# First mixer of a two-block layer: the gate row's sums and the gate on the output projection move from GpSimd to VectorE

## The chip, the cores and the metric

The kernel runs on one core of a Trainium2 chip. The metric is the device time of one execution in microseconds, as the median of several runs. The engines are TensorE (matmul and its weight loads), VectorE, ScalarE (called ACT in the rows), GpSimd (POOL) and SyncE (SP), whose queue issues nearly all DMA transfers of weights. Each engine works through its own instructions in order and waits for the others by semaphores.

## What is computed

Two transformer blocks run one after the other on 256 tokens of 1024 features, all in float32. The first block modulates: six rows of 1024 come from one condition vector, and two of them are gates on the outputs of the block's two halves.

```python
def first_block(x, c, w_ada, b_ada, ...):
    mod = (silu(c) @ w_ada + b_ada)                 # 1024 x 6144 weights
    shift_m, scale_m, gate_m, shift_f, scale_f, gate_f = split(mod, 6)
    h = rms_norm(x, g_mix) * (1 + scale_m) + shift_m
    x = x + gate_m * hybrid_mixer(h, ...)           # two attentions, 8 heads each
    h = rms_norm(x, g_ffn) * (1 + scale_f) + shift_f
    x = x + gate_f * hierarchical_moe(h, ...)       # 32 experts, 2 per token
    return rms_norm(x, g_final)

def hybrid_mixer(h, w_in, b_forget, g_out_a, g_out_b, w_out):
    proj = h @ w_in                                 # 1024 x 2896
    ...
    o = concatenate([rms_norm(oa, g_out_a), rms_norm(ob, g_out_b)])
    return o @ w_out                                # 1024 x 1024
```

`oa` is an attention with a choice of 64 keys per query (an indexer makes the choice), `ob` a forgetting attention. The second block has a recurrent mixer and a dense feed-forward part.

## The kernel before, in words

Tokens lie in two blocks of 128 (t = 0, 1). Products that need accuracy are made from two parts, `hi` (rounded by ACT) and `lo` (the rest, by VectorE), in three matmuls (`mm3`); `split` makes the parts of a weight piece of 128x1024.

Weights come in pieces of 1 MB through a ring of eleven buffers (`raw`), by loads that SP issues in the order of the program: `load` (L53) and, for the modulation rows, `ada_piece` (L125), four pieces `wada` for each row. The order is the string at L207: a digit is a piece of that modulation row (0 and 1 are loaded before), "bq", "aq", "kv" and so on are pieces of w_in. Behind it come the four pieces of w_out (`wob` for the forgetting attention's half, `woa` for the other) and then the expert weights (`load_experts`), which go into this ring and two smaller ones. The smaller ones share space with the first mixer's tiles, so the last loads before the experts begin wait for the mixer's end; the twenty-first waits for the buffer of `xn2`, the normed input of the experts.

The modulation rows 0 to 4 are made by TensorE (`ada`, L328). Row 5, `gate_f`, is made otherwise (`gate_row`, L360): for each of the eight halves of its pieces, ACT scales 128x1024 weights by the column of silu(c) in place (L366), and GpSimd adds them to `modrow[:, 1]` (L367); `gate_row_end` (L370) sums over the partitions with a matmul of ones, within the first expert unit. `modrow[:, 0]` is `gate_m`. The gate is put on the weights of the output projection: `gate_out` (L378) multiplies the w_out pieces by `modrow[:, 0]` on GpSimd (L382), `wob` in `gate_out(0)` and `woa` in `gate_out(1)`. `proj_out` (L575) then makes the products of each half, and `add` (L585) scales the result by the attention's norm and adds it to `xt`, the running sum.

The work of the first mixer is written as generators, one for each job, and a string at L879 says in which order their steps are written out: "B" and "C" are the forgetting attention on token block 0 and 1 (`attn`, L694, with the softmax in L732 to L747), "D" and "E" the other attention, "2", "3", "4" the modulation rows on TensorE, "5" `gate_row`, "G" and "H" `gate_out`, "o" and "p" the output projection's halves, lower case letters projections. A scheduler then lays out each engine's instructions ahead of time by this order as priority; an instruction that is ready may come ahead of earlier ones that are not. Only SP's loads and what is marked so keep the order of the program. `mm` has one line for all matmuls (L100), and `hilo` one for each part (L86, L87), so groups are told apart by their tiles.

Of the kernel before, what the change touches and what calls it, by code (L numbers as in the profile page):

```python
# [7 lines left out]
FT = mybir.dt.float32  # L8
# [3 lines left out]
AF = mybir.ActivationFunctionType  # L12
OP = mybir.AluOpType
# [3 lines left out]
T = 256  # L17
# [15 lines left out]
def tile_block(ctx: ExitStack, tc: tile.TileContext, A, out):  # L33
    nc = tc.nc
    pe, act, dve, pool = nc.tensor, nc.scalar, nc.vector, nc.gpsimd
# [10 lines left out]
    def bank(shape, name):  # L46
        return ps.tile(shape, FT, name=name, tag="bank")
# [22 lines left out]
    def load_cols(name, dname, width, c0, n, j0, nj):  # L70
        return load(name, (nj, n), dram(dname, j0 * width + c0,
                                        [[8 * width, 128], [width, nj], [1, n]]))
# [3 lines left out]
    def held(ins):  # L76

        if holding:
            tc.keep_in_program_order(ins)
        return ins  # L80
# [8 lines left out]
    def split(src, name, n, eng=dve):  # L89
        hi = spl.tile([128, 1024], FR, name=name + "h", tag="hi")[:, :n]  # L90
        lo = spl.tile([128, 1024], FR, name=name + "l", tag="lo")[:, :n]
        hilo(hi, lo, src, eng)
        return hi, lo
# [16 lines left out]
    def mm3(o, lh, rh, start, stop):  # L110
        mm(o, lh[0], rh[0], start, False)
        mm(o, lh[0], rh[1], False, False)
        mm(o, lh[1], rh[0], False, stop)
# [11 lines left out]
    def ada_piece(v):  # L125
        w = wada.setdefault(v, [])
        q = len(w)
        w.append(load(f"wada{v}_{q}", (2, D), dram("w_ada", 2 * q * 6 * D + v * D,
                                                   [[8 * 6 * D, 128], [6 * D, 2], [1, D]])))
# [6 lines left out]
    xt = const.tile([128, 2, D], FT, name="xt")  # L136
    modrow = const.tile([128, 2, D], FT, name="modrow")
# [5 lines left out]
    a1 = p1.enter_context(tc.tile_pool(name="a1", bufs=1, side="right"))  # L143
# [8 lines left out]
    bkT, bv = bkv[:, 0], bkv[:, 1].rearrange("p a b -> p (a b)").rearrange("p (t n) -> p t n", t=2)  # L152
# [51 lines left out]
    later = {"bq": w_bq, "bk": w_bk, "bv": w_bv, "aq": w_aq}  # L204
    for v in (2, 3, 5, 4):
        wada[v] = []
    for name in 'bq bq bk 2 2 bk bv bv 3 5 aq kv 2 2 3 3 aq 3 5 5 5 4 4 4 4'.split():  # L207
        if name == "kv":
            w_kv = load_cols("wkv", "w_in", WIN, 512, 256, 0, 8)
        elif name in COLS:  # L210
            c0, n = COLS[name]
            k = len(later[name])
            later[name].append(load_cols(f"win{c0}_{k}", "w_in", WIN, c0, n, 4 * k, 4))
        else:
            ada_piece(int(name))
    wo = []

    def wob_load():
        for i in range(2):
            wo.append(load(f"wob{i}", (2, D), dram("w_out", (512 + 256 * i) * D,  # L220
                                                  [[D, 128], [128 * D, 2], [1, D]])))
# [4 lines left out]
    W, last = {}, []  # L226
# [94 lines left out]
    cs = const.tile([128, 8], FT, name="cs")  # L321
# [38 lines left out]
    def gate_row():  # L360

        m = modrow[:, 1]
        for q in range(4):
            for jj in range(2):
                w = wada[5][q][:, jj]
                act.activation(w, w, AF.Copy, scale=cs[:, 2 * q + jj:2 * q + jj + 1])  # L366
                pool.tensor_tensor(m, m, w, op=OP.add)  # L367
            yield

    def gate_row_end():  # L370
# [4 lines left out]
        for half in range(2):  # L375
            act.activation(m[:, 512 * half:512 * half + 512], b[half], AF.Copy)

    def gate_out(part_):  # L378

        for r in range(4):  # L380
            w = wo[2 * part_ + r // 2][:, r % 2]
            pool.tensor_tensor(w, w, modrow[:, 0], op=OP.mult)  # L382
        yield


    def rstd_of(ssq, n, name, post=None):
        t = small.tile(list(ssq.shape), FT, name=name + "s", tag="ns")
        held(act.activation(t, ssq, AF.Sqrt, bias=epsc[:, 0:1], scale=1.0 / n))
        r = post if post is not None else small.tile(list(ssq.shape), FT, name=name + "r", tag="nr")
        dve.reciprocal(r, t)  # L390
        return r

    def sumsq(src, name, junk):
        s = small.tile([128, 1], FT, name=name)
        act.activation(junk, src, AF.Square, accum_out=s)
        return s
# [38 lines left out]
    for t in range(2):  # L435
        r = rstd_of(sumsq(xt[:, t], "ss", xn[:, t]), D, "rs")
# [121 lines left out]
    def turn_x(t):  # L558
        b = [bank([128, 4, 128], "p_tr") for _ in range(2)]
        for j in range(8):  # L560
            held_pe(pe.transpose(b[j // 4][:, j % 4], xt[:, t, j::8], ident))
        return b
# [4 lines left out]
    def first_half_first(n, last):  # L567

        if n == last - 2:
            return [(n, 0)]  # L570
        if n == last - 1:
            return [(n, 0), (n - 1, 1), (n, 1)]
        return [(n, 0), (n, 1)]

    def proj_out(part_, oh, ol, rs):  # L575
        acc, kept = [], []
        for r in range(4):
            def cut(r=r):
                return split(wo[2 * part_ + r // 2][:, r % 2], "wo", 1024)

            def prod(hi, lo, r=r):
                if r == 0:
                    acc.extend([bank([128, 512], "p_wo") for _ in range(2)] for _ in range(2))
                kept.append((hi, lo))
                def add(t, half):  # L585
                    hs = slice(half * 512, half * 512 + 512)
                    held(dve.scalar_tensor_tensor(xt[:, t, hs], acc[t][half], rs[:, t:t + 1], xt[:, t, hs],
                                                  op0=OP.mult, op1=OP.add))

                if part_ and r == 3:  # L590
                    holding.extend([True, True])
                for r_, t in first_half_first(r, 4):
                    ts = slice(t * 128, t * 128 + 128)
                    hi, lo = kept[r_]
                    for half in range(2):
                        hs = slice(half * 512, half * 512 + 512)
                        mm3(acc[t][half], (oh[:, r_, ts], ol[:, r_, ts]), (hi[:, hs], lo[:, hs]), r_ == 0, r_ == 3)
                        if part_ and r == r_ == 3:
                            if t == 0:
                                add(t, half)  # L600
                            elif half == 0:
                                trb.append(turn_x(0))
                if r == 3:
                    if part_:
                        del holding[:]
                        add_outs.append(add)
                    else:
                        for t in range(2):
                            for half in range(2):
                                add(t, half)  # L610

            yield cut, prod
# [210 lines left out]
    def flush():  # L823
        while pend:
            pend.pop(0)()
# [6 lines left out]
    def loads1():  # L832
        wob_load()
        woa_load()
        load_experts(len(RING) - RING.count(3))
        yield

    def turn_rows():
        p_rows = bank([128, 64], "p_rows")
        pe.transpose(p_rows, rows, ident[:64, :64])  # L840
        dve.tensor_copy(cols, p_rows)
        yield

    def rstd_b():
        oa.extend([a1.tile([128, 4, T], FR, name="oaT", tag="iq"), a1.tile([128, 4, T], FR, name="oaL", tag="bq")])
        rstd_of(ssq[:, 2:4], 512, "rb_", rsb)
        yield

    def rstd_a():
        rstd_of(ssq[:, 0:2], 512, "ra_", rsa)  # L850
        yield

    def router_weights():
# [3 lines left out]
        for j in range(8):  # L857
# [15 lines left out]
            "a": proj_fm(w_aq, aqT, 0.125, perm=True), "n": proj_kv(), "o": proj_out(0, obT, obL, rsb),  # L873
            "F": forget(), "X": indexer(1), "Y": indexer(0), "B": attn("b", 0), "C": attn("b", 1),
            "D": attn("a", 0), "E": attn("a", 1), "2": ada(2), "3": ada(3), "4": ada(4), "5": gate_row(),
            "G": gate_out(0), "H": gate_out(1), "T": turn_rows(), "W": loads1(), "R": rstd_b(), "S": rstd_a(),
            "Z": router_weights()}
    p_ = None
    for c in "iiqikqqFqXFXbbYYbbvY5TXXF22XY25XY5v5vYXYXv2BWBa2aaBYBnGB3BC33CCCC3BCanB3C!CR4D4D4D4E4DDDEoEHoEoDEoDEEESZpppp":  # L879
        if c == "!":  # L880
            flush()
        elif c == "p":
            if p_ is None:
                p_ = proj_out(1, *oa, rsa)
            main([next(p_)], 0)
        elif c.islower():
            main([next(work[c])], 0)
        else:
            next(work[c])
# [475 lines left out]
    q = const.tile([128, 2], FT, name="q")  # L1365
# [475 lines left out]
    q = const.tile([128, 2], FT, name="q5")  # L1841
# [36 lines left out]
    q = small.tile([128, 2], FT, name="ss5q")  # L1878
# [28 lines left out]
    for half in range(2):  # L1907
# [10 lines left out]
                                  op0=OP.mult, op1=OP.mult))  # L1918
# [31 lines left out]
```

## Time and profile before

| | |
|---|---|
| timed runs, median (lowest to highest of 3) | 741.2 us (740.72 to 742.93) |
| the profiled execution | 738.99 us, span 737.2 us |
| TensorE busy | 660.9 us, 90% of the span |
| VectorE busy | 402.3 us, 55% |
| ACT busy | 311.4 us, 42% |
| GpSimd busy | 88.9 us, 12% |
| moved by DMA | 196.94 MB, mean 267 GB/s |

The profile is one execution of the program. Its span runs from the first to the last instruction; the execution's own time is longer by what lies around it. A busy share is an average over stages with different limits: the first mixer takes the first 186 us, the experts the stretch up to some 414 us, the second block the rest. "Releaser" names what ended a wait. Where GpSimd's busy time stands, 42.5 us of it are the sums and gate products of this change (19.9 for L367, 11.8 and 10.8 for L382).

### The profile page before, as it was taken

The page shows a single profiled execution, that of the slowest core. Times are in us where ns is not written, and L with a number is a line of the kernel's source. Part 1 is how long each engine was busy: PE and PEld are TensorE (multiplying, and loading weights), DVE is VectorE, ACT ScalarE, POOL GpSimd, SP SyncE. Part 2 cuts the span into 40 slices and gives each one's busy share as a digit, 9 for nine tenths or more (in the row PEclk, how much of TensorE's full clock was granted, in tenths as well). Part 3 has the DMA queues.
Part 4 walks back from the last instruction along what each step waited for, and adds up shares of the span by engine and source line. Part 5 has one row for each costly group of instructions (what it writes and reads, how often), then busy time and mean ns, then how long its engine had stood idle before and what let it go on. Part 6 is the DMA issues. An engine that isn't in the chain of part 4 may idle for free. (4 is left out here: it accounts for less than half of the span.)

```text
span 737.2 us, 13263 instructions
## 1 busy us (share of the span) xinstructions
PE 660.9 (90%) x5489; PEld 510.4 (69%) x5489; DVE 402.3 (55%) x737; ACT 311.4 (42%) x513; POOL 88.9 (12%) x87
## 2 busy tenths in 40 slices
PE   5799996999899775998876989999999999999996
PEld 1498774877765333444442489987899999898994
DVE  2367978575663230423312269959676555555555
ACT  1446556564741010201110177685455444444445
POOL 7010309910000000000000063010000000000001
PEclk9899998999989998999988999999999999999999
DMA  9999779995639899998999999653445555550001
GB/s 342 372 382 359 257 273 292 307 405 206 261 133 421 322 421 415 405 397 332 422 418 420 374 370 387 212 172 116 138 149 172 172 192 201 177 199 34 1 1 57
DMA packets 69203, 196.94 MB, mean 267 GB/s; under 512 B 7550, under 2 KB 33219, under 8 KB 57350
## 3 DMA queue, kind: packets, MB, share of 16 engines
q1 hardware_dynamic: 67558, 195.30, 70.5%
q8 instruction: 53, 0.87, 0.5%
q10 hardware_dynamic: 1216, 0.30, 0.2%
q0 software_dynamic: 352, 0.28, 0.1%
q14 instruction: 24, 0.20, 0.1%
HBM read 194.81 MB, written 1.05 MB: 266 GB/s over the span
## 5 line engine op out<-in xcount | busy, mean ns | idle before, releaser
L100 PE MATMUL p_gu<-Xl,wguh 128*128 128x256 f32 x352 | 99.8, 284 | 0.0
L100 PE MATMUL p_gu<-Xh,wgul 128*128 128x256 f32 x352 | 99.3, 283 | 0.0
L100 PE MATMUL p_gu<-Xh,wguh 128*128 128x256 f32 x352 | 98.9, 283 | 0.1
L100 PEld LDWEIGHTS p_gu<-Xl,wguh 128*128 128x128 f32 x352 | 67.5, 192 | 0.5
L100 PEld LDWEIGHTS p_gu<-Xh,wguh 128*128 128x128 f32 x352 | 67.1, 192 | 0.7 <-ACT Xh L1379 0.4
L100 PEld LDWEIGHTS p_gu<-Xh,wgul 128*128 128x128 f32 x352 | 67.4, 192 | 0.3 <-DVE wgul L87 0.2
L100 PE MATMUL p_gu<-eg,xg 128*32 128x256 f32 x576 | 41.8, 416 | 15.3 <-PEq L1296 9.5
L87 DVE TENSOR_TENSOR wdnl<-wdn,wdnh 128x1024 fp32r<-128x1024 f32 x22 | 27.0, 1225 | 32.4 <-ACT wdnh L86 32.4
L100 PEld LDWEIGHTS p_gu<-eg,xg 128*32 128x32 f32 x576 | 19.7, 118 | 36.0 <-issue 24.4
L1149 DVE TENSOR_TENSOR sl<-sl,p_gu 128x256 f32<-128x256 f32 x9 | 3.8, 422 | 69.2 <-ACT sl L1148 69.2
L1148 ACT ACTIVATE sl<-p_gu 128x256 f32<-128x256 f32 x9 | 3.5, 384 | 87.9 <-PE p_gu L100 87.9
L100 PE MATMUL p_w<-hTh,wih 128*128 128x256 f32 x128 | 37.7, 297 | 2.5 <-ACT wih L86 2.5
L100 PE MATMUL p_dn<-ed,aT 128*32 128x512 f32 (+2 forms) x304 | 34.5, 573 | 5.2 <-ACT aT L1156 5.0
L86 ACT ACTIVATE wdnh<-wdn 128x1024 fp32r<-128x1024 f32 x22 | 23.3, 1058 | 36.5 <-PE p_gu L100 35.9
L87 DVE TENSOR_TENSOR wgul<-wup,wguh 128x1024 fp32r<-128x1024 f32 x22 | 27.0, 1226 | 21.3 <-ACT wguh L86 20.2
L1066 ACT ACTIVATE xg<-p_xg,modcol,af 128x128 f32<-128x128 f32 x36 | 15.6, 462 | 53.2 <-DVE xg L1068 53.0
L87 DVE TENSOR_TENSOR wgul<-wgt,wguh 128x1024 fp32r<-128x1024 f32 x22 | 27.0, 1225 | 19.8 <-ACT wguh L86 19.8
L86 ACT ACTIVATE wguh<-wgt 128x1024 fp32r<-128x1024 f32 x22 | 23.3, 1061 | 33.7 <-PE p_gu L100 18.2
L100 PE MATMUL p_w<-Xh,w2h 128*128 128x256 f32 x128 | 37.0, 289 | 0.5 <-ACT w2h L86 0.4
L100 PE MATMUL p_w<-Xh,w2l 128*128 128x256 f32 x128 | 36.3, 285 | 1.1 <-DVE w2l L87 0.6
L100 PE MATMUL p_w<-hTl,wih 128*128 128x256 f32 x128 | 36.9, 289 | 0.0
L100 PE MATMUL p_gu<-eu,xg 128*32 128x256 f32 x576 | 35.2, 379 | 1.9 <-DMA eu<-in_w_up_dram 1.9
(625 smaller groups left out, 1645.0 us busy)
## 6 DMA issues: line engine op xcount, KB each, us to landing
eg<-in_w_gate_dram SPq DMA_DIRECT2D x32, 1024.0 KB
eu<-in_w_up_dram SPq DMA_DIRECT2D x32, 1024.0 KB
ed<-in_w_down_dram SPq DMA_DIRECT2D x28, 1024.0 KB
wada<-in_w_ada_dram SPq DMA_DIRECT2D x24, 1024.0 KB
w<-in_w_in_dram SPq DMA_DIRECT2D x11, 1024.0 KB
wgt<-in_w_gate_up_dram SPq DMA_DIRECT2D x11, 1024.0 KB
wup<-in_w_gate_up_dram SPq DMA_DIRECT2D x11, 1024.0 KB
wdn<-in_w_down_dram SPq DMA_DIRECT2D x11, 1024.0 KB
```

Of the source, the lines that this page charges most:

```text
L86: held(act.activation(hi, src, AF.Copy))
L87: held(eng.tensor_tensor(lo, src, f32(hi), op=OP.subtract))
L100: held_pe(pe.matmul(o, lhsT, rhs, start=start, stop=stop, skip_group_check=True))
L1066: act.activation(xg[:, j], b[:, jj], AF.Identity, bias=bf_[:, j:j + 1], scale=af[:, j:j + 1])
L1148: act.activation(st.s[:st.n], st.b[:st.n, 0:256], AF.Silu)
L1149: dve.tensor_tensor(st.s[:st.n], st.s[:st.n], st.b[:st.n, 256:512], op=OP.mult)
```

## The change

The eight sums of row 5 are made by VectorE in one fused operation each (weights times the column of silu(c), plus the sum so far); ACT's scaling and GpSimd's addition are gone. The gate on the forgetting attention's half of w_out is gone ("G"); its output is multiplied by the gate row as it is taken from the accumulators, in `add`, by a fused operation into a new tile `gated`, and a second operation adds that to `xt`. The gate products on the other half stay on the weights, on VectorE, in two steps ("H" twice). In the order of loads the pieces of row 5 come last, behind those of row 4, and in the order of work the steps "5" come behind those of "4", in the stage of the second attention.

```diff
-    for name in 'bq bq bk 2 2 bk bv bv 3 5 aq kv 2 2 3 3 aq 3 5 5 5 4 4 4 4'.split():
+    for name in 'bq bq bk 2 2 bk bv bv 3 aq kv 2 2 3 3 aq 3 4 4 4 4 5 5 5 5'.split():
...
                 w = wada[5][q][:, jj]
-                act.activation(w, w, AF.Copy, scale=cs[:, 2 * q + jj:2 * q + jj + 1])
-                pool.tensor_tensor(m, m, w, op=OP.add)
+                dve.scalar_tensor_tensor(m, w, cs[:, 2 * q + jj:2 * q + jj + 1], m, op0=OP.mult, op1=OP.add)
             yield
...
-    def gate_out(part_):
+    def gate_out():
 
         for r in range(4):
-            w = wo[2 * part_ + r // 2][:, r % 2]
-            pool.tensor_tensor(w, w, modrow[:, 0], op=OP.mult)
-        yield
+            w = wo[2 + r // 2][:, r % 2]
+            dve.tensor_tensor(w, w, modrow[:, 0], op=OP.mult)
+            if r % 2:
+                yield
...
                 def add(t, half):
                     hs = slice(half * 512, half * 512 + 512)
-                    held(dve.scalar_tensor_tensor(xt[:, t, hs], acc[t][half], rs[:, t:t + 1], xt[:, t, hs],
-                                                  op0=OP.mult, op1=OP.add))
+                    if part_:
+                        held(dve.scalar_tensor_tensor(xt[:, t, hs], acc[t][half], rs[:, t:t + 1], xt[:, t, hs],
+                                                      op0=OP.mult, op1=OP.add))
+                    else:
+                        g_ = a1.tile([128, 512], FT, name="gated", tag="fin", bufs=3)
+                        dve.scalar_tensor_tensor(g_, acc[t][half], rs[:, t:t + 1], modrow[:, 0, hs],
+                                                 op0=OP.mult, op1=OP.mult)
+                        dve.tensor_tensor(xt[:, t, hs], xt[:, t, hs], g_, op=OP.add)
...
-            "G": gate_out(0), "H": gate_out(1), "T": turn_rows(), "W": loads1(), "R": rstd_b(), "S": rstd_a(),
+            "H": gate_out(), "T": turn_rows(), "W": loads1(), "R": rstd_b(), "S": rstd_a(),
...
-    for c in "iiqikqqFqXFXbbYYbbvY5TXXF22XY25XY5v5vYXYXv2BWBa2aaBYBnGB3BC33CCCC3BCanB3C!CR4D4D4D4E4DDDEoEHoEoDEoDEEESZpppp":
+    for c in "iiqikqqFqXFXbbYYbbvYTXXF22XY2XYvvYXYXv2BWBa2aaBYBnB3BC33CCCC3BCanB3C!CR4D45D45D45EH45DDDEoHEoEoDEoDEEESZpppp":
```

## Rows read from the trace of the kernel before

**Rows 1.** Chain that ended last: start us, us, what.

```profile
414.54 7.51 DMA w<-in_w_in_dram
```

**Rows 2.** Stretches: busy us (instructions) of PE, PEld, DVE, ACT, POOL; clock, DMA, GB/s.

```profile
130.00:190.00 60.00, 57.94 (x456) 45.61 (x453) 37.74 (x65) 32.74 (x71) 20.41 (x12) 0.96 0.80 291
...
200.00:213.00 13.00, 10.32 (x72) 6.58 (x74) 10.19 (x20) 6.61 (x9) 0.00 (x0) 0.74 0.01 3
214.00:400.00 186.00, 151.48 (x1777) 79.89 (x1769) 54.49 (x118) 22.13 (x59) 1.03 (x2) 0.95 0.96 395
```

**Rows 3.** Waits of SP's queue: line, waited for; us in total, times, longest.

```profile
SPq L252 <- DVE xn L1007: 23.5, 1, 23.5
```

**Rows 4.** SP's queue in order of time: start us, us, line, out<-in, count.

```profile
92.02 0.89 SPq L63 DMA_DIRECT2D wada<-in_w_ada_dram  x2
...
96.97 1.24 SPq L63 DMA_DIRECT2D wada<-in_w_ada_dram  x2
...
111.48 5.06 SPq L63 DMA_DIRECT2D wob<-in_w_out_dram  x2
...
213.88 2.06 SPq L252 DMA_DIRECT2D ed<-in_w_down_dram  x4
```

**Rows 5.** TensorE in order of time; in brackets idle us before and its releaser.

```profile
98.63 1.98 PE L100 MATMUL p_row<-part,selh 128*128 128x512 f32 x4 [1.49 <-DVE part L344]
...
120.01 0.28 PE L100 MATMUL p_w<-hTh,wil 128*128 128x256 f32 x1
...
127.13 1.94 PE L754 MATMUL p_pt<-ident,prob 128*128 128x128 f32 x8 [6.84 <-DVE brc L746]
...
153.24 1.10 PE L100 MATMUL p_col<-selh,part 128*64 128x1 f32 x32 [0.94 <-ACT part L351]
```

**Rows 6.** Stretches, columns as in rows 2, about TensorE's longest wait.

```profile
120.00:130.00 10.00, 3.16 (x21) 2.65 (x21) 9.90 (x8) 3.93 (x14) 9.84 (x5) 0.71 0.80 186
...
124.00:130.00 6.00, 2.87 (x18) 2.57 (x20) 5.97 (x3) 1.59 (x6) 6.00 (x3) 0.51 1.04 212
130.00:132.00 2.00, 2.00 (x20) 1.67 (x17) 0.96 (x2) 0.92 (x2) 2.00 (x1) 0.77 1.11 229
```

**Rows 7.** Two lines of VectorE: ns min/median/max, first and last start us, forms.

```profile
L738 DVE TENSOR_TENSOR bbi<-cumq,bmx x6: 132/972/2247, 97.8 to 121.3; 128x2 f32<-128x2 f32 x4, 128x4 f32<-128x4 f32 x2
...
L747 DVE TENSOR_TENSOR prob<-prob,brc x2: 3168/3264/3360, 123.6 to 127.1; 128x1024 f32<-128x1024 f32 x2
L747 DVE TENSOR_TENSOR aP<-aP,arc x2: 693/693/693, 151.5 to 152.9; 128x512 f32<-128x512 f32 x2
L747 DVE TENSOR_TENSOR prob<-prob,arc x2: 1221/1224/1226, 157.2 to 159.5; 128x1024 f32<-128x1024 f32 x2
```

**Rows 8.** VectorE in order of time, three of its instructions.

```profile
87.50 0.15 DVE L1253 TENSOR_TENSOR lm<-cols 128x4 f32<-128x4 f32 x1
...
114.78 1.38 DVE L737 TENSOR_TENSOR bmx<-bmx,cumq 128x2 f32<-128x2 f32 x1
...
127.11 3.17 DVE L747 TENSOR_TENSOR prob<-prob,brc 128x1024 f32<-128x1024 f32 x1
```

**Rows 9.** GpSimd in order of time.

```profile
111.25 14.65 POOL L367 TENSOR_TENSOR modrow<-modrow,wada 128x1024 f32<-128x1024 f32 x6 [24.09 <-ACT wada L366]
125.86 11.77 POOL L382 TENSOR_TENSOR wob<-wob,modrow 128x1024 f32<-128x1024 f32 x4
137.59 10.81 POOL L382 TENSOR_TENSOR woa<-woa,modrow 128x1024 f32<-128x1024 f32 x4
```

**Rows 10.** ACT in order of time.

```profile
112.60 4.25 ACT L366 ACTIVATE wada<-wada,cs 128x1024 f32<-128x1024 f32 x4
118.72 0.47 ACT L741 ACTIVATE prob<-p_sc,bbi 128x256 f32<-128x256 f32 x1 [1.87 <-DVE bmx L737]
```

**Rows 11.** Groups of VectorE by line: busy us, mean ns, then idle time before.

```profile
L1611 DVE SCALAR_TENSOR_TENSOR a__8943<-a__8943,la 128x1024 f32<-128x1024 f32 x1 | 1.2, 1216 | 0.0
...
L1167 DVE SCALAR_TENSOR_TENSOR yf<-p_dn,cslot,modrow 128x512 f32<-128x512 f32 x17 | 12.8, 751 | 29.4 <-PE p_dn L100 29.1
```

## The prediction, made before the changed kernel was run

> **What bounds the kernel now.** I read the chain that ended last, then the order and the waits of SP's queue, then TensorE and VectorE in the first mixer.
>
> The end of the program hangs on the expert weights: the chain comes out of the last expert load, runs through the second block's first weights from 414.54 us [rows 1] and is then nearly all matmuls. From 214 to 400 us the DMA engines are 0.96 busy [rows 2]: the length of that stretch is given by bytes. It starts when SP can issue again. The fifth load of the second expert unit waits 23.5 us for the buffer that holds the normed input [rows 3], which L1007 frees at 213.9 us [rows 4]. Ahead of that DMA does nothing for 13 us [rows 2]. So the transfers have slack until the first mixer is over and none afterwards: if the mixer ends X us earlier, everything behind it comes X us earlier.
>
> What sets the mixer's end is TensorE. Between 36 and 186 us it hardly ever waits; three waits are worth naming [rows 5]. The largest, 6.84 us ahead of 127.13, is for VectorE: the softmax of the forgetting attention's second query block. In 120 to 130 us VectorE is busy for 9.90 of 10 us, GpSimd for 9.84, TensorE for 3.16 [rows 6].
>
> VectorE has not much to do there. L738, on a few elements a row, takes 132 ns at best and up to 2247 ns, and L747 on 128x1024 takes 3.26 us here and 1.22 us for the same shape in the other attention [rows 7]; only here does GpSimd run beside it, from 111.25 to 148.4 us without a gap [rows 9]. The long ones in this softmax, seven instructions in six rows of the timeline, of which the first and the last are shown [rows 8], take 1.38, 1.94, 1.85 (two), 2.25, 3.36 and 3.17 us: 13.95. Five at some 0.16 and two at 1.22 would be 3.2. So for 10.7 us of this chain VectorE is held up while GpSimd works. The trace shows the coincidence, not the cause; that is a rival below.
>
> **GpSimd's work goes.** Eight sums and eight gate products, 2.4 to 2.9 us each [rows 9], leave the engine. GpSimd itself is on no path; the gain is VectorE's held time. The softmax without it: its first reductions start at 113.6, when the scores are there; four of them at 0.68 and eight small operations at 0.16 end at 117.6; the eight exponentials, 0.47 from start to start, run from 115.2 to 119.0; the first normalization, 0.17 + 1.22, ends at 119.0, the second at 120.6. TensorE has other work until 120.3 [rows 5]. Of the 6.84 us some 6.8 go, less 0.1 for the second normalization. ACT's scalings matter too: four of them run until 116.85, and the first exponential started at 118.72 only because VectorE was late [rows 10]. Had they stayed, they would be next in line, 1.7 us behind 115.2. They leave as well.
>
> **The clock comes with it.** The granted clock is 0.51 in 124 to 130 us and 0.77 in the two after, behind TensorE's idle time [rows 6]; that is the lower of its two levels, 1.2 instead of 2.4 GHz. TensorE works from 127.13, so up to 131 us it takes 3.9 us for what takes half of that at the upper level: 1.9 us. Without the idle time that goes too. Together 6.8 - 0.1 + 1.9 = 8.6 us.
>
> **Small gains.** 1.49 us ahead of 98.63 (VectorE late with a row's sum, soon after the first of GpSimd's sums) and 0.94 us ahead of 153.24 (ACT late) [rows 5], with some 1.5 us of lower clock behind the second. Between 0 and 3.9; I take 0.6, since VectorE's new work falls in the same stretch as the larger part.
>
> **VectorE's new work.** Eight sums with the scale folded in: the nearest row is L1611, a fused operation of that shape at 1.22 us [rows 11]: 9.8 us. Four gate products at the 1.22 of L747 [rows 7]: 4.9 us. On the output of the first half, four fused operations at 0.75 (L1167, same kinds of operands [rows 11]) in place of four of about that length, and four additions of 128x512 at 0.69 [rows 7]: 2.8 us. Together 17.5 us. From 130 to 190 us VectorE is busy for 37.74 of 60 us [rows 2]: 22.3 free for 17.5, and held time comes off besides. Its gaps are filled from far ahead: L1253, which stands in the third expert unit, ran at 87.50 [rows 8]. What is on nobody's path costs nothing, but each new piece can hold a ready softmax operation for up to its own 1.22 us. Bounds of the cost: 0 and 17.5. I take 1.4, one or two pieces of twelve in TensorE's way, because TensorE's queue had other work all the time from 131 to 186 us, but for 0.94 us.
>
> A page speaks against this part. The Trainium skill (Perfetto Trace Analysis, Optimizing Scalar/DVE Operations) says that where VectorE is saturated, moving work off it, even to GpSimd, can make sense, with the warning that the two share a read port. By that rule the change goes the wrong way in 120 to 130 us, where VectorE is full; it would give the third rival below. By the rows, 10.7 us of that fullness is not VectorE's own work.
>
> **The order of loads.** The fourth row's weights (a column set) now come ahead of the gate row's. Number and size stay. In SP's queue eight loads come one place earlier, the column set four, the row's first piece 12 places later. In the ring of eleven buffers that frees one in which the piece sat from 50 to 87 us; TensorE waits for no load there, so I cost it at nothing. Afterwards up to eight buffers hold modulation weights at once, the column set until TensorE reads it (142 to 148.5 us before), the row until VectorE does. w_out, issued from 111.48 us [rows 4], and the first experts behind it may then wait some 10 us. The cover is DMA's idle time ahead of 213.9, 13 us, less the 8 by which the mixer ends earlier, and some idle time about 175 us. I cost it at nothing too, with the cover nearly used; once it is gone, each further microsecond counts in full, as the queue is in order and every later load stands behind.
>
> **The sum.** 8.6 + 0.6 - 1.4 = 7.8 us off the mixer's end and so off the whole. The profiled execution took 738.99 us (span 737.2, and 1.8 around it): 731.2. It lies 2.2 us below the timed runs' median of 741.2; against the median the forecast is 733.4 us.
>
> **Rivals.**
> - The forecast: the stall and its slow clock go, the new work hides. 731 to 736.5, chance 0.61.
> - More comes back: the small gains in full and nothing paid for the new work, 8.6 + 3.9 = 12.5, 728 to 731. For it: TensorE is the bound nearly everywhere. Against: the new work lies in those stretches. 0.10.
> - VectorE takes over: sums and products stand ahead of softmax operations in the remaining attentions. With half of its duration for each of the twelve large pieces that is 7.3 us; from a third of that up the time is 736 to 740. For it: 37.7 + 17.5 of 60 us. 0.16.
> - Slower: VectorE stands still for weights. The gate row's weights take the last four places of the modulation loads, issued from 96.97 us on before [rows 4], and VectorE works in order. If one sum stands ahead of a softmax while its weights' buffer comes free only after the products on the column set, at 142 us, softmax and TensorE wait with it. It decides once that wait passes 8.6 us; with 12 us the time is 744.6. For it: eight of eleven buffers held. Against: ACT's scalings at 112.60 [rows 10] stand 18 to 20 us behind the issue of their loads (92 us) [rows 4], so the order was laid out with late arrivals in mind. 0.08.
> - It doesn't do what it says: the long VectorE rows are not GpSimd's doing, or another step is as late. 741. Against: the same shape at 1.22 us without GpSimd. 0.05.
>
> **How the numbers follow.** A measurement of this kernel tells 0.3%, 2.2 us, from no change: 739.0 to 743.4. Faster: 0.61 + 0.10 + 0.10 of VectorE's case = 0.81. Same: its other 0.06 + 0.05 = 0.11. Slower: 0.08. The range leaves out the slower case, the one without effect and half of the larger gain, 0.18 together: 730 to 740.
>
> **What would show it.** Right: L738 and L747 of the forgetting attention at 0.16 and 1.22 us; no wait ahead of the transposes of its second block; a granted clock of 1.0 from 120 to 135 us; SP's restart (213.88 us) near 206, and every later row shifted by as much. Wrong: VectorE busy for over 9 of 10 us from 120 to 180 us with TensorE waiting for it, a sum that waits for its weights, or SP's restart where it was.

## The result, and the profile of the changed kernel

The changed kernel takes 732.1 us (median; 731.0 to 733.1) against 742.0 for the kernel before on the same chip: ratio 0.987, interval 0.985 to 0.989. A second group of runs gave 731.1 against 741.1, ratio 0.987 (0.985 to 0.990). The forecast was 733.4 us and 7.8 us less; it became 9.9 less.

In the changed kernel's listing the sums are L366, the gate products L381, the gated output L592 and L594; in the forgetting attention's softmax the small operations are L743 and L744 (L737 and L738 before), the reductions L738, the normalization L753 (L747 before). TensorE's transposes of the softmax are L760, the transposes of the mixer's output L561, and L1013 frees the normed input, xn2. In the experiments the same lines lie up to ten further on or back; the tiles' names stay.

The stretches of [rows 2] and [rows 6], of the kernel after, columns as there:

```profile
120.00:130.00 10.00, 9.70 (x123) 9.34 (x122) 8.39 (x11) 4.24 (x9) 0.00 (x0) 1.00 1.05 253
130.00:190.00 60.00, 57.52 (x395) 45.02 (x393) 44.63 (x100) 38.22 (x78) 2.01 (x5) 0.97 0.89 352
206.00:392.00 186.00, 152.82 (x1765) 82.27 (x1757) 54.12 (x114) 21.80 (x59) 1.02 (x2) 0.94 0.96 394
```

From 120 to 130 us TensorE goes from 3.16 to 9.70 us busy, the granted clock from 0.71 to 1.00. From 130 to 190 VectorE is busy for 6.9 us more, of 22 that were free; the stretch now also holds the router's first ten. The stretch of expert loads is as full as it was (0.96); it only starts earlier.

The softmax of the second block on VectorE in order of time (start us, us, line), answering to [rows 8]:

```profile
116.02 1.23 DVE L753 TENSOR_TENSOR prob<-prob,brc 128x1024 f32<-128x1024 f32 x1
117.17 1.28 DVE L366 SCALAR_TENSOR_TENSOR modrow<-wada,cs,modrow 128x1024 f32<-128x1024 f32 x1
...
118.48 1.28 DVE L366 SCALAR_TENSOR_TENSOR modrow<-wada,cs,modrow 128x1024 f32<-128x1024 f32 x1
119.68 1.22 DVE L753 TENSOR_TENSOR prob<-prob,brc 128x1024 f32<-128x1024 f32 x1
```

The normalizations take 1.23 and 1.22 us where they took 3.36 and 3.17. Two of the new sums stand between them, so the second one starts at 119.68; in the kernel with the new orders alone (below), whose softmax starts 0.15 us later and has no sums in it, it starts at 117.99.

All of TensorE's waits between 60 and 190 us (line, waited for; us in total, times, longest), first of the kernel before, then of the one after:

```profile
PE p_pt L754 <- DVE brc L746: 6.8, 1, 6.8
PE p_row L100 <- DVE part L344: 1.5, 1, 1.5
PE p_lg L100 <- DVE h L951: 1.1, 1, 1.1
PE p_lft L636 <- DVE lf L632: 1.0, 1, 1.0
PE p_col L100 <- ACT part L351: 0.9, 1, 0.9
```

```profile
PE p_pt L760 <- DVE aP L753: 1.4, 1, 1.4
PE p_lg L100 <- DVE h L957: 1.1, 1, 1.1
PE p_lft L642 <- DVE lf L638: 1.0, 1, 1.0
PE p_pt L760 <- DVE prob L753: 0.3, 1, 0.3
```

The wait of 6.8 us and both smaller ones (1.5 and 0.9) are gone; 0.3 us is left ahead of the same transposes, and one wait of 1.4 us in the other attention is new. SP's queue, answering to [rows 4] (213.88) and [rows 1] (414.54):

```profile
205.46 1.94 SPq L252 DMA_DIRECT2D ed<-in_w_down_dram  x4
...
407.45 12.93 SPq L63 DMA_DIRECT2D w<-in_w_in_dram  x8
```

The mixer's transposes start at 176.49 us instead of 186.48 (10.0 earlier), SP starts again 8.4 earlier, the second block's weights come 7.1 earlier, and the profiled execution is 8.0 shorter (731.0 against 738.99).

### The profile page after: what moved, and what is told of

It reads as the page before. It is cut to its first block, busy times and chain, and to the rows that moved or that the text cites. A ratio compares the mean times of both kernels' runs of the same rounds, so it can differ in the third digit from the quotient of the medians.

```text
span 729.3 us, 13242 instructions
## 1 busy us (share of the span) xinstructions
PE 661.0 (91%) x5489; PEld 511.3 (70%) x5489; DVE 400.2 (55%) x753; ACT 303.5 (42%) x505; POOL 46.1 (6%) x71
## 5 line engine op out<-in xcount | busy, mean ns | idle before, releaser
L100 PE MATMUL p_gu<-eg,xg 128*32 128x256 f32 x576 | 43.9, 434 | 16.6 <-PEq L1302 9.2
L100 PE MATMUL p_w<-hTh,wil 128*128 128x256 f32 x128 | 36.7, 291 | 0.0
```

The source lines that it names most:

```text
L100: held_pe(pe.matmul(o, lhsT, rhs, start=start, stop=stop, skip_group_check=True))
```

## The experiments

**Is it GpSimd at all?** The changed kernel with GpSimd made busy again beside the softmax, at the scores of the forgetting attention's second block, with work that nobody needs: either it reads two SBUF tiles, or it only writes. The target is a mask that is no longer used. The other engines have the same instructions in the same order.

```
+        if kind == "b" and t == 1:
+            junk_ = negsel.rearrange("p a b -> p (a b)")
+            for _ in range(15):
+                pool.tensor_tensor(junk_, modrow[:, 0], xt[:, 0], op=OP.mult)   # dummy_read
+            # or: for _ in range(38): pool.memset(junk_, 0.0)                     dummy_write
```

Reading, expected:

> The changed kernel with fifteen products of 128x1024 added on GpSimd, two inputs in SBUF each, written over a mask that nobody reads any more, from the moment the forgetting attention's second block has its scores. Nobody waits for them, and every other engine has the same instructions in the same order. Theory (GpSimd at work on SBUF inputs holds up VectorE's operations on two SBUF inputs, and that was the loss): the softmax is late again, most of the gain goes, 738 to 742 us. Rivals (the new order of loads and steps, or ACT freed of its scalings, is the gain): 732.

Writing, expected:

> As the one before, but GpSimd only writes in that time: 38 fills of the same mask, about the same busy time. If any GpSimd work holds VectorE up, 738 to 742 us; if it takes GpSimd reading SBUF (the Trainium skill, SBUF - State Buffer, Who interferes with whom, says that a VectorE instruction with two SBUF inputs contends with a GpSimd instruction that reads SBUF, not with one that only writes), 732.

Measured: with reading 756.2 us, ratio to the kernel before 1.023 (1.019 to 1.028), far above the 738 to 742 that were expected; with writing 730.1 us, 0.987 (0.983 to 0.991), the changed kernel's own ratio (its mixer's transposes start at 177.5 us, 1.0 later). Reading, first GpSimd, then VectorE, both in order of time, and the stretch:

```profile
112.57 44.55 POOL L734 TENSOR_TENSOR negsel<-modrow,xt 128x1024 bf16<-128x1024 f32 x15 [64.77 <-PE p_sc L100]
```

```profile
120.02 2.25 DVE L748 TENSOR_TENSOR bbi<-cumq,bmx 128x2 f32<-128x2 f32 x1
122.39 3.37 DVE L757 TENSOR_TENSOR prob<-prob,brc 128x1024 f32<-128x1024 f32 x1
125.67 3.37 DVE L366 SCALAR_TENSOR_TENSOR modrow<-wada,cs,modrow 128x1024 f32<-128x1024 f32 x1
```

```profile
120.00:130.00 10.00, 4.10 (x25) 3.47 (x26) 9.95 (x6) 3.04 (x13) 9.76 (x4) 0.53 0.63 148
```

Writing, the same three views:

```profile
112.22 38.30 POOL L734 MEMSET negsel<- 128x1024 bf16 x38 [64.67 <-PE p_sc L100]
```

```profile
114.27 0.16 DVE L748 TENSOR_TENSOR bbi<-cumq,bmx 128x2 f32<-128x2 f32 x1
115.55 1.22 DVE L757 TENSOR_TENSOR prob<-prob,brc 128x1024 f32<-128x1024 f32 x1
```

```profile
120.00:130.00 10.00, 9.70 (x123) 9.34 (x122) 8.39 (x12) 4.09 (x9) 9.43 (x11) 1.00 1.06 241
```

GpSimd is about as busy in both (9.76 and 9.43 of these 10 us). Only where it reads SBUF do the rows of the kernel before return: a 128x2 operation at 2.25 us instead of 0.16, the normalization at 3.37 instead of 1.22, a clock of 0.53, and now the new sums suffer as well (3.37 instead of 1.28). This settles the rival "it doesn't do what it says": what held VectorE up is GpSimd's reading. (The two kinds of dummy work also differ in length, some 3.0 and 1.0 us each, but a hold of even 1.0 us would show on operations of 0.16, and none does.) The Trainium skill (SBUF — State Buffer, Who interferes with whom) says that a VectorE instruction with two SBUF inputs contends with a GpSimd instruction that reads SBUF and not with one that only writes; these runs agree.

The loss is larger than expected. GpSimd now reads for 44.55 us (37.2 in the kernel before), beside a VectorE that has the sums as well: TensorE waits 13.0 us in two pieces ahead of the softmax's transposes where the kernel before has 6.8, two waits of 2.8 and 2.9 us follow, and the mixer's transposes start at 203.4 us. The expectation counted the old loss only.

**One part of the change at a time.** Three kernels built from the one before: the sums on VectorE only; the gate products only (four on VectorE, and the first half's gate on its output); the new orders of loads and steps only.

```
sums_only (in the kernel before)
-                act.activation(w, w, AF.Copy, scale=cs[:, 2 * q + jj:2 * q + jj + 1])
-                pool.tensor_tensor(m, m, w, op=OP.add)
+                dve.scalar_tensor_tensor(m, w, cs[:, 2 * q + jj:2 * q + jj + 1], m, op0=OP.mult, op1=OP.add)
gates_only: gate_out(), add() and "H" of the change; sums and both orders as before
order_only: both order strings of the change, with "G" kept; all work as before
```

> The kernel before with only the sums moved to VectorE, orders as before; all gate products stay on GpSimd. Six sums stand inside the second softmax, and the gate products start once w_out is there, at about 115 us, so the normalizations are held up as well. Theory: 740 to 746, no gain. If the sums alone were the loss: 732 to 735.

> The kernel before with only the gate products changed (the first half's on the output, the second half's on VectorE), orders as before; scalings and sums stay on ACT and GpSimd, which is then free from 126 us on. Theory: the six sums at 111 to 126 us still hold the softmax up, TensorE still waits some 7 us, only the later held operations are freed: 739 to 742. If the gate products were the loss: 733 to 735.

> The kernel before with only the orders changed: the gate row's weights last, its steps behind the fourth row's; the scalings stay on ACT, sums and gate products on GpSimd. If the order is the gain: 732. Theory: GpSimd's gate products on the first half now lie in the softmax instead of its sums and hold VectorE up as well, and the sums and the second half's products run on into the other attention: 740 to 748.

Measured: sums only 745.3 us, ratio 1.005 (1.002 to 1.008), a little slower; gate products only 740.3, 0.999 (0.997 to 1.001), no change; orders only 746.9, 1.009 (1.006 to 1.012), slower. All three times lie in the ranges that the theory gave. In us of a time of 741 that is +3.4, -1.0 and +6.6, and together they make -9.6. No part brings a gain by itself that is clear of the noise. The traces say why: in the first two GpSimd still reads SBUF beside the forgetting attention's softmax; in the third it does not, but there its products come too late for w_out.

With the gate products gone, GpSimd's first row, and VectorE's two normalizations:

```profile
111.46 14.64 POOL L367 TENSOR_TENSOR modrow<-modrow,wada 128x1024 f32<-128x1024 f32 x6 [24.11 <-ACT wada L366]
```

```profile
123.82 3.36 DVE L754 TENSOR_TENSOR prob<-prob,brc 128x1024 f32<-128x1024 f32 x1
...
127.30 1.23 DVE L754 TENSOR_TENSOR prob<-prob,brc 128x1024 f32<-128x1024 f32 x1
```

GpSimd's sums end at 126.1 us. The normalization that starts before that takes 3.36 us, the one after it 1.23, and TensorE has waited its 6.8 us by then. With the sums gone instead, the gate products run beside the same softmax, from 119.03 to 140.2 us, and six sums on VectorE stand ahead of and between its reductions: TensorE's wait grows.

```profile
119.03 10.41 POOL L381 TENSOR_TENSOR wob<-wob,modrow 128x1024 f32<-128x1024 f32 x4 [71.35 <-DMA wob<-in_w_out_dram]
```

```profile
PE p_pt L753 <- DVE prob L746: 9.9, 2, 8.2
```

How much of this is GpSimd can be read against the kernel of the next experiment (old_order): it has the same sums in the same softmax and no gate products on GpSimd, and there these waits are 2.8 and 0.7 us instead of 8.2 and 1.7.

With the new orders alone the sums come later. That clears the forgetting attention (VectorE's normalization at 117.99 takes 1.23 us, and no transposes of it wait), and GpSimd reads from 118.86 to 161.6 us, beside the other attention's softmax, where small operations are held:

```profile
118.86 15.55 POOL L367 TENSOR_TENSOR modrow<-modrow,wada 128x1024 f32<-128x1024 f32 x6 [71.31 <-ACT wada L366]
```

```profile
L734 DVE TENSOR_SCALAR abi<-amx x6: 157/1526/2345, 137.3 to 162.2; 128x2 f32<-128x2 f32 x4, 128x4 f32<-128x4 f32 x2
```

```profile
PE p_col L100 <- ACT part L351: 8.7, 1, 8.7
```

```profile
142.38 5.69 POOL L382 TENSOR_TENSOR wob<-wob,modrow 128x1024 f32<-128x1024 f32 x2
```

```profile
145.80 1.06 ACT L86 ACTIVATE woh<-wob 128x1024 fp32r<-128x1024 f32 x1 [5.66 <-DMA eg<-in_w_gate_dram]
```

The wait of 8.7 us has another cause than the 6.8: the held operations are over by 142.4 us, and VectorE then has nothing to do for 3.3 us. ACT's queue stands at the split of a w_out piece (`woh<-wob`), which starts at 145.80, as GpSimd's product on that piece ends (145.77; the load that the row names as releaser is none of this piece). The exponentials and the modulation row's `part` stand behind it. So here GpSimd's own lateness is on the path, with the sums ahead of the gate products in its queue, and not VectorE's held time; the expectation's 740 to 748 us came true by another way than it named. Of the 6.6 us that this kernel loses, only 1.7 are there at the mixer's transposes (188.2 against 186.48); it loses more behind them, which is told below (the late xn2).

**The orders of loads and steps, undone in the changed kernel.** Both order strings as they were, the gate products' step put where the change has it:

```
-    for name in 'bq bq bk 2 2 bk bv bv 3 aq kv 2 2 3 3 aq 3 4 4 4 4 5 5 5 5'.split():
+    for name in 'bq bq bk 2 2 bk bv bv 3 5 aq kv 2 2 3 3 aq 3 5 5 5 4 4 4 4'.split():
```

> The changed kernel with the loads and the steps of the gate row in the order of before; the sums are still VectorE's. My prediction put the order at nothing: 732. Against it: in this kernel six of the eight sums (1.28 us each) stand between the reductions of the forgetting attention's second softmax, so VectorE gives that softmax 7.7 us late in place of GpSimd; TensorE has other work for some of it: 735 to 739. If the order is all of the gain: 742.

Measured: 732.0 us, ratio 0.990 (0.986 to 0.994): by the time, the 732 of the prediction. Six of the eight sums now stand in the second block's softmax, three ahead of its first reduction and three between the reductions, and TensorE waits again; VectorE, and TensorE's waits:

```profile
110.98 3.92 DVE L366 SCALAR_TENSOR_TENSOR modrow<-wada,cs,modrow 128x1024 f32<-128x1024 f32 x3
114.81 0.68 DVE L738 TENSOR_REDUCE bmx<-p_sc 128x2 f32<-128x512 f32 x1
115.42 1.27 DVE L366 SCALAR_TENSOR_TENSOR modrow<-wada,cs,modrow 128x1024 f32<-128x1024 f32 x1
```

```profile
PE p_pt L760 <- DVE bbi L744: 2.8, 1, 2.8
```

The mixer's transposes start at 178.5 us, 2.0 later than in the changed kernel. The two intervals overlap, so the 2 us rest on one trace and not on the ratio (the kernel with GpSimd writing, which has the new orders, was 1.0 later too). The orders keep six sums out of this softmax; that they gain time by it is not shown.

**What does VectorE's new work cost?** Four kernels built from the changed one. The first cuts sums and gate products to 8 of 1024 columns and leaves out the gate of the first half's output. The second cuts the sums alone; their row is used only behind the first router. The third doubles: ahead of each of the twelve large pieces stands one more operation of its shape, the maximum of the weight tile with itself. The fourth gives ACT its scalings back and leaves VectorE the additions.

```
no_new_work
-                dve.scalar_tensor_tensor(m, w, cs[:, 2 * q + jj:2 * q + jj + 1], m, op0=OP.mult, op1=OP.add)
+                dve.tensor_scalar(m[:, 0:8], w[:, 0:8], 1.0, None, op0=OP.mult)
-            dve.tensor_tensor(w, w, modrow[:, 0], op=OP.mult)
+            dve.tensor_tensor(w[:, 0:8], w[:, 0:8], modrow[:, 0, 0:8], op=OP.mult)
-                    if part_:
+                    if True:
no_sums: m[:, 0:8] and w[:, 0:8] in the sums' line
double_work: dve.tensor_tensor(w, w, w, op=OP.max) ahead of each sum and each gate product
act_scale
+                act.activation(w, w, AF.Copy, scale=cs[:, 2 * q + jj:2 * q + jj + 1])
+                dve.tensor_tensor(m, m, w, op=OP.add)
```

> The changed kernel without VectorE's new work: the sums and the gate products each touch 8 of 1024 columns, and the first half's output is added without the gate, so most of the gate row's sum and of the gate on the mixer's output is left out. Theory (the new work hides, 1.4 us of 17.5 in the way): 730 to 732. Rival (VectorE has become a bound of the mixer): 722 to 728.

> The changed kernel, with the eight sums for the last modulation row done on 8 of their 1024 columns (the row is wrong after that; it is used only behind the first mixture's router, so the same experts get the same tokens, which was not so where the gate products were cut). It takes 8 sums of 1.28 us = 10.2 us from VectorE and leaves the gate products. If VectorE's new work is hidden but for a tenth, as the prediction had it (1.4 of 17.5 us), the time is that of the changed kernel less 0.8 us, and the transposes behind the mixer stay within 1 us of 176.5. If it costs what the kernel without new work gained over the changed one (4 of 17.5 us), it is 2.3 us less and the transposes start at 174 or before. Four overflow branches of experts run, as in the changed kernel (576 products of eg with xg).

> The changed kernel, with one more VectorE instruction of the same shape (the weight tile's maximum with itself, which changes nothing) ahead of each of the eight sums and four gate products: 12 times 1.22 us = 14.6 us more on VectorE. Hidden but for a tenth: 1.2 us slower than the changed kernel. At 4 of 17.5 us: 3.3 us slower. If VectorE is by now the engine that sets the mixer's end: up to 14.6 us slower, back to the time of the kernel before or above it.

> The changed kernel, but the scaling stays on ACT (eight of 1.14 us) and VectorE only adds (1.22 in place of 1.28). The prediction had ACT's scalings in the exponentials' way; in the new order they come behind them. If ACT has time there: 731 to 733. If it is in the way: 734 to 737.

With next to no new work: 727.3 us, ratio 0.982 (0.979 to 0.985), 4 us below the changed kernel and in the range of the rival (722 to 728). These 4 us are not the price of the new work: the same group of expert products, of the kernel after and of this one,

```profile
L100 PE MATMUL p_gu<-eg,xg 128*32 128x256 f32 x576 | 43.9, 434 | 16.6 <-PEq L1302 9.2 <-issue 6.0 <-ACT xg L1072 1.2
```

```profile
L100 PE MATMUL p_gu<-eg,xg 128*32 128x256 f32 x512 | 40.2, 441 | 19.5 <-PEq L1302 11.2 <-issue 6.9 <-ACT xg L1072 1.4
```

has 512 products instead of 576. They come 64 to an expert unit: eight units, and in the changed kernel one overflow branch besides (one, not the four of the expectation of no_sums). Without the gate the router sees other numbers, no unit overflows, and the expert stage is shorter: from SP's restart to the second block's first weights it takes 196.6 us (209.66 to 406.21), where each of the twelve other profiles has 200.7 to 204.3 with the same number of bytes. SP even starts again 4.2 us later than in the changed kernel (209.66 against 205.46), so nothing of what the mixer gains here arrives at the end by that way. The price of the new work is to be read ahead of the router: the mixer's transposes start at 174.4 us instead of 176.5, 2.1 earlier, and the waits of 0.3 and 1.4 us are gone.

Without the sums, and with the same 576 products, the kernel is slower, not faster: 734.1 us, ratio 0.991 (0.989 to 0.994), against 731.1 for the changed kernel in the same group. TensorE's waits, and GpSimd's first write into xn2, which marks that its place in SBUF is free, of this kernel:

```profile
PE p_lg L100 <- DVE h L957: 3.4, 1, 3.4
...
PE p_pt L760 <- DVE aP L753: 1.4, 1, 1.4
```

```profile
178.71 0.10 POOL L910 MEMSET xn<- 128x1 f32 x1 [9.26 <-PE p_wo L100]
```

Taking 10.2 us of sums off VectorE moves the mixer's transposes by 0.4 us, and to the later side (176.9): the sums were hidden, but for the 0.3 us. The 1.4 us stay, so they belong to the gate products. What makes the kernel slower stands behind the mixer: xn2 is free at 178.71, after the last product of w_out (178.65), where in the changed kernel it was free at 176.02, while the last of these products and the transposes were still to come. The first copy for the router comes late, TensorE waits 3.4 us for it in place of 1.1, and SP starts again at 208.0 instead of 203.7 (205.5 in the first profile of the changed kernel, which had the same lower clock from 180 to 190 us as this one, 0.83). The same wait of 3.4 to 3.7 us is in three more kernels: no_new_work, order_only and act_scale. GpSimd's write waits for a later product there; what decides for which one it waits was not isolated.

With the work doubled: 738.9 us, ratio 0.998 (0.996 to 1.000), 7.8 us slower than the changed kernel for 14.6 us more on VectorE. TensorE's waits:

```profile
PE p_pt L760 <- DVE aP L753: 7.4, 1, 7.4
...
PE p_wo L100 <- DVE wol L87: 1.5, 1, 1.5
```

The transposes start at 185.8 us, 9.4 later. VectorE is busy for 12.00 of 12 us from 142 to 154 us, where the changed kernel has 11.02. The first 17 us of new work cost about 2, the next 14.6, at the same places, cost 9.4 at the mixer's end: the cover is nearly used up. This is the rival "VectorE takes over"; where between these two sizes it begins was not measured.

With ACT's scalings back: 738.1 us, ratio 0.995 (0.992 to 0.998), where 731 to 733 or 734 to 737 was expected: the median is above both, the interval (735.2 to 739.6 us of a time of 741.2) reaches into the second. Its ten runs go from 733.4 to 743.8, and the profiled one is the slowest, so what the trace shows is more than the median lost. The waits are those of the next fence; xn2 is late here too.

```profile
PE p_lg L100 <- DVE h L958: 3.4, 1, 3.4
PE p_pt L761 <- DVE aP L754: 2.0, 1, 2.0
```

The mixer's transposes start at 179.9 us, 3.4 later. The scalings do not disturb the forgetting attention (TensorE is 10.00 us busy from 120 to 130); they come in the way in the other one, where VectorE's split of w_out waits 2.8 us for ACT's copies (0.3 in the changed kernel), the wait of 1.4 becomes 2.0, and the granted clock is 0.72 from 142 to 154 us. The rest of this execution's loss is xn2's wait and a clock of 0.64 from 180 to 206 us. By the ratios 5.8 of the 9.6 us go when the scalings come back, though GpSimd reads nothing beside the softmax: so in this order more than half of the gain needs ACT freed as well as GpSimd. How much of it is the scalings' time and how much the late xn2 was not separated.

## Why the prediction held, point by point

**The end hangs on the expert loads, and X passes on.** Right for this change. The profile of the changed kernel is 10.0 us earlier at the mixer's end, 8.4 at SP's restart, 7.1 at the second block's weights and 8.0 at the end. The 1.6 us between the first two were lost in the router, which the prediction did not name: from 180 to 190 us the granted clock was 0.83 in the profiled execution, while the kernel before had 1.00 through its router (180 to 200). In a repeat of the changed kernel it is otherwise:

```profile
180.00:190.00 10.00, 10.00 (x72) 9.87 (x72) 5.58 (x32) 9.15 (x17) 0.00 (x0) 1.00 0.96 404
```

Here the clock is 1.00, SP starts again at 203.72 (10.2 earlier than before), and the profiled execution takes 728.8 us, 10.2 less. It is the fastest of its group; the medians differ by 9.9 and 10.0 us in the two groups, which says the same: X passes on. But bytes alone do not set the length of the expert stretch, as the prediction had it: with one overflow branch less and the same bytes it is some 5 us shorter (196.6 against 201.3 and 202.0 us in the two profiles of the changed kernel), and the chain that ended last goes through the last expert loads in the repeat and only through expert products (from 398.02 us) in the first profile.

**The idle time and its clock, 8.6 us.** Right in kind: 6.8 became 0.3, and the granted clock is 1.00 in every 2 us from 108 to 182. The prediction left 0.1 us ahead of the transposes; the other 0.2 are the two sums between the normalizations. The 1.9 us for the clock are not confirmed as a size (see the sum below).

**The small gains, 0 to 3.9, taken at 0.6.** This is the term that was mis-sized. Both waits went entirely (1.5 and 0.9), and so did the low clock behind the second (0.83 from 150 to 160 us before, 1.00 after, which is up to 1.7 us): up to 4.1, just above the upper bound. The prediction had set the new work against them as if it fell into the same gaps. Part of the first wait hangs on the orders: with the old ones 0.8 of its 1.5 us is still there (sums_only, old_order).

**VectorE's new work, 0 to 17.5, taken at 1.4.** About right in size. The durations are as estimated or close (sums 1.28 instead of 1.22, gate products 1.21, output 0.73 and 0.68). TensorE waits 0.3 us for the sums and 1.4 for the gate products, 1.7; the kernel without the work puts it at 2.1. So with these terms the sum is 8.6 - 0.2 + 4.1 - 1.4 = 11.1 against the 10.0 seen at the mixer's end. The waits are not what is short: TensorE's idle time from 60 us to these transposes falls from 10.3 to 2.7 us, by the 7.6 that the listed waits give. Its busy time falls by 2.4 (116.2 to 113.8), where the two clock terms, 1.9 and 1.7, make 3.6. So they were counted some 1.2 us too high, or other products took longer; that was not isolated. The prediction's three terms gave 7.8: it was 2 us short, mostly by the small gains.

**The orders of loads, at nothing.** By the time, right: undone, 732.0 us. By the trace they are not neutral: undone, they put six sums into the softmax, and the mixer ends 2.0 us later in that one execution. The prediction weighed them only by when weights come, not by where the planned sums land on VectorE. The danger that it did name, loads that hold up w_out and the experts, did not come: the loads from 120 to 160 us are denser than before (DMA 1.02 busy against 0.93), and DMA stands still for 16 us ahead of SP's restart.

**ACT's scalings.** "Had they stayed, they would be next in line, 1.7 us": kept in the new order, they cost 3.4 us at the mixer's end in the slowest of ten runs, and in the other attention.

**The rivals.** GpSimd's reading as the cause of the held softmax is shown by reading against writing. "VectorE waits for weights" fell: no sum waited for its weights. The advice of the Trainium skill that was weighed (Perfetto Trace Analysis, Optimizing Scalar/DVE Operations) is that taking work off a saturated VectorE may make sense, and that between VectorE and GpSimd it might not help, as they share a read port. Read as a reason against the change the first half fails here: VectorE's busy time fell from 402.3 to 400.2 us although some 17 us of work were added. The second half is what the case shows. What speaks for caution is the run with the work doubled.

## What to carry to other kernels

Before VectorE is called saturated, compare the durations of one shape with and without GpSimd beside it: a 128x2 operation that takes 2 us here and 0.16 there is not work but a wait. In this kernel no part of the move helped alone (the three parts cost or gained +3.4, -1.0 and +6.6 us, all of them together -9.6), for two reasons: GpSimd still read beside the softmax, or its products came late. So measure such a move as a whole before dropping it for what its parts do. And a price that is read from a kernel with work left out holds only if the data that steer later branches, and the waits behind the work, stay as they were: read it at the first stage behind the work, not at the end.

## What the runs showed of the hardware

- Which of VectorE's instructions are held while GpSimd reads: those of 128x2 with two SBUF inputs (0.15 to 2.25 us), 128x1024 ones (1.22 to 3.37), fused ones (1.28 to 3.37) and also the small L734 of order_only, which has one SBUF tile and a number (0.16 to 2.35). Not held: reductions out of PSUM (0.68 for 128x512 beside GpSimd or not) and 128x512 operations with one PSUM input (0.69).
- GpSimd's writing alone cost VectorE nothing: 38 fills of 128x1024 in 38.3 us, and all rows stayed as in the changed kernel.
- The granted clock of a stretch can differ between two executions of one kernel: 0.83 and 1.00 from 180 to 190 us, with 1.7 us between the two restarts of SP.
